# A table places the first stage's instructions, and the bias split moves from the expert stage into that stage

## The chip, the cores and the metric

The kernel runs on one core of a Trainium2 chip. The metric is the device time of one execution in microseconds; three timed runs are shown, and one more execution was profiled.

## What is computed

One layer of a diffusion trunk over 256 latent tokens and 256 context tokens of width 1024: a bidirectional chunked gated DeltaNet (8 heads of 128, chunks of 64) as the token mixer, then a mixture of 32 experts, of which each token takes 4, then a final normalisation. Everything is float32. The reference, cut to what matters here:

```python
hx = modulate(rmsnorm(x, norm1_g[i]), mx[0], mx[1])
hc = modulate(rmsnorm(ctx, norm1_g[i]), mc[0], mc[1])
o_c, s_f, s_b = bidir_gated_delta(qc, kc, vc, gc, bc, zero_state, zero_state)
o_x, _, _ = bidir_gated_delta(qx, kx, vx, gx, bx, s_f, s_b)
x = x + mx[2] * gdn_output(o_x, zx, gdn_norm_g[j], gdn_w_out[j])
hx2 = modulate(rmsnorm(x, norm2_g[i]), mx[3], mx[4]).reshape(-1, d)

def moe(h, w_r, b_r, w_gu, b_gu, w_dn, b_dn):
    ...
    for e in range(N_EXPERTS):
        y = y + comb[:, e:e + 1] * clamped_swiglu_expert(h, w_gu[e], b_gu[e], w_dn[e], b_dn[e])
```

An expert is `h @ w_gu + b_gu` (1024 to 2048), a clamped SwiGLU, and `@ w_dn + b_dn` (1024 to 1024), so its weights are 12 MiB, and all 32 experts are 384 MiB. They are read once.

## The kernel before

**First stage (the mixer).** The work is cut into operations on a head or a group of four heads, and the list `ORDER` names the order in which they are written out: `k`, `v`, `q`, `z` project the tokens for one head (matmuls L264, L265, L426 on weights that were split into a rounded part and a rest, lines 78 and 83), `um`, `ia`, `ib`, `ic` build and invert the chunks' triangular matrices, `st` is one step of the scan over chunks for four heads, `norm` and `op` make the output and add it to the tokens `x1`, `ada` computes the gates from the conditioning vector (L693). The scheduler of the language places instructions by their position in the program; an engine runs what it is given in order. `inv_c(4)` is the last part of the inverse for the second four heads: 16 small matmuls (L599), copies of their result into `y1c`, 16 more matmuls on that (L608), and copies into `U`. In a step of the scan (`step`), PE multiplies the state `St` (L624), DVE forms `R` (L634), PE forms the new values (L642) and the update (L660), DVE adds it to `St` (L666), PE multiplies within the chunk (L672), and DVE adds this to `vs` (L676, L678). The output matmuls are L756; the last row transposes of the gates, L700, end the stage. `rowG`, the gain of the second normalisation, is loaded early into memory of the pool `ep` and transposed there (L386).

**Second stage (experts).** Tokens are routed (L892 to L957), and the experts follow one after another. Each has six weight tiles of 2 MiB, four for gate and up and two for down; all 192 are loaded by `issue` on SP's queue (L780) into a ring of nine slots, seven of which reuse memory of the first stage: a load waits until the last use of what lay there. Expert 0's gate and up matmuls are L995, the down matmuls L1030. An expert with more than 64 tokens takes an additional pass. Around it, and once for each quarter of expert 0, all engines pass a block boundary (L1181, L1221), so none gets ahead of the others there.

**The bias.** The matmuls that add a bias need it as three bfloat16 parts (`bgu`, `bdn`, 96 rows). `bias(i)`, written out after the routing, loads it three times into 32 rows each (L930, on ACT's queue), and splits it with casts on ACT (L931, L934, L936) and subtractions on DVE (L932, L935).

## Time and profile before

| | us |
|---|---|
| timed runs, median (lowest to highest of 3) | 1426.8 (1426.25 to 1428.42) |
| profiled execution | 1418.68 |
| its span | 1416.9 |
| PE busy in the span | 1269.2 (90%) |
| DVE busy | 497.9 (35%) |
| ACT busy | 363.7 (26%) |
| POOL busy | 214.5 (15%) |
| HBM read | 454.05 MB, 321 GB/s over the span |

Times within the kernel are those of the profiled execution, from the span's start. A busy share is an average over two stages with different limits, so the rows below are read by stretches.

### The profile page before, as it was taken

What the parts mean: (1) busy time and instruction counts of PE and PEld (TensorE: products, weight loads), DVE (VectorE), ACT (ScalarE), POOL (GpSimd) and SP (SyncE); (2) the same over time, 40 slices, a digit from 0 to 9 for tenths busy, and PEclk for the clock granted to TensorE, in tenths of its full rate; (3) what the DMA queues carried; (4) which work ended last, traced back from release to release, by engine and by line L of the source; (5) the groups of instructions that cost most, each with busy time, mean ns of one, the idle gap of its engine ahead of it and who ended that gap; (6) DMA issues with size and microseconds to landing.
All of it is one profiled execution on the core that took longest, in us unless ns stands there. A gap on an engine that the chain in (4) does not pass through costs nothing. (4 is left out here: it accounts for less than half of the span.)

```text
span 1416.9 us, 18778 instructions
## 1 busy us (share of the span) xinstructions
PE 1269.2 (90%) x6815; PEld 629.3 (44%) x6815; DVE 497.9 (35%) x1076; ACT 363.7 (26%) x811; POOL 214.5 (15%) x204
## 2 busy tenths in 40 slices
PE   4997899889996899999899999999999899987995
PEld 2565667678753333333343334333333333332331
DVE  4569989856553121120112221121211102111123
ACT  3375453435435311111120211211111111111112
POOL 3043334315310000100000001000100001000011
PEclk9999899979998899999999999999999999999998
DMA  9633334323667699999996999999999999999992
GB/s 257 211 90 89 105 108 117 123 86 105 242 287 268 272 428 426 426 426 425 427 424 250 399 427 426 426 426 426 426 426 427 427 426 427 426 427 422 425 426 98
DMA packets 88582, 457.11 MB, mean 323 GB/s; under 512 B 7940, under 2 KB 57289, under 8 KB 63857
## 3 DMA queue, kind: packets, MB, share of 16 engines
q1 hardware_dynamic: 85392, 453.68, 79.8%
q8 instruction: 94, 1.54, 0.4%
q10 hardware_dynamic: 3041, 1.44, 0.4%
q14 instruction: 55, 0.45, 0.1%
HBM read 454.05 MB, written 1.05 MB: 321 GB/s over the span
## 5 line engine op out<-in xcount | busy, mean ns | idle before, releaser
L995 PE MATMUL psG<-w,hTe 128*64 128x512 f32 x1024 | 283.7, 620 | 42.3 <-DMA w<-in_moe_w_gu_dram 25.0
L995 PE MATMUL psU<-w,hTe 128*64 128x512 f32 x1024 | 277.9, 607 | 0.0
L1030 PE MATMUL psY<-w,aT 128*64 128x512 f32 x1024 | 225.2, 592 | 0.1
L1216 POOL TENSOR_TENSOR YAB<-y,YAB 64x512 fp32r<-64x512 f32 x62 | 78.4, 1264 | 887.5 <-ACT YAB L1215 885.2
L1211 DVE SCALAR_TENSOR_TENSOR y<-psY,cw,gate 128x512 f32<-128x512 f32 x32 | 24.0, 751 | 354.1 <-PE psY L1030 354.1
L995 PEld LDWEIGHTS psU<-w,hTe 128*64 128x64 f32 x1024 | 85.4, 141 | 134.6 <-issue 131.6
L1030 PEld LDWEIGHTS psY<-w,aT 128*64 128x64 f32 x1024 | 73.5, 137 | 140.4 <-issue 137.7
L995 PEld LDWEIGHTS psG<-w,hTe 128*64 128x64 f32 x1024 | 66.7, 137 | 147.6 <-issue 109.9
L1005 DVE TENSOR_SCALAR g<-psG 128x512 f32<-128x512 f32 x33 | 34.3, 1041 | 237.4 <-PE psG L995 232.8
L1215 ACT CAST YAB<-y 64x512 fp32r<-64x512 f32 x64 | 39.4, 616 | 291.9 <-DVE y L1211 152.9
L264 PE MATMUL pp<-hh,w 128*128 128x256 f32 (+1 forms) x240 | 86.6, 376 | 13.1 <-DVE w L78 5.1
L265 PE MATMUL pp<-hl,w 128*128 128x256 f32 (+1 forms) x240 | 84.7, 368 | 0.0
L1034 DVE TENSOR_TENSOR x<-x,psX 128x512 f32<-128x512 f32 x68 | 43.7, 683 | 108.7 <-PE psX L1089 106.8
L979 ACT ACTIVATE hTe<-psX,adac,A 128x128 f32<-128x128 f32 x128 | 48.1, 456 | 127.4 <-PE psX L977 127.4
L83 POOL TENSOR_TENSOR w<-w 128x1024 fp32r<-128x1024 f32 x24 | 57.6, 2399 | 109.0 <-ACT w L78 29.3
L977 PEld LDWEIGHTS psX<-oh,xn 128*128 128x128 f32 x512 | 59.5, 192 | 25.0 <-issue 12.2
L445 DVE SCALAR_TENSOR_TENSOR acc<-pp,colB,acc 128x508 f32<-128x508 f32 (+3 forms) x96 | 62.5, 653 | 19.7 <-ACT acc L433 18.9
L977 PE MATMUL psX<-oh,xn 128*128 128x128 f32 x512 | 65.4, 281 | 0.6 <-DVE oh L968 0.6
L264 PEld LDWEIGHTS pp<-hh,w 128*128 128x128 f32 x240 | 49.6, 207 | 24.4 <-DVE w L78 5.8
L426 PE MATMUL pp<-hh,w 128*128 128x256 f32 (+1 forms) x240 | 53.7, 352 | 0.6 <-POOL w L83 0.6
L265 PEld LDWEIGHTS pp<-hl,w 128*128 128x128 f32 x240 | 49.6, 207 | 6.1 <-issue 0.5
L1077 ACT CAST ST<-psX 128x256 fp32r<-128x256 f32 x16 | 5.9, 371 | 170.0 <-PE psX L1075 170.0
(400 smaller groups left out, 1449.7 us busy)
## 6 DMA issues: line engine op xcount, KB each, us to landing
w<-in_moe_w_gu_dram SPq DMA_DIRECT2D x128, 2048.0 KB, 19.7
w<-in_moe_w_dn_dram SPq DMA_DIRECT2D x64, 2048.0 KB, 21.1
w<-in_gdn_w_in_dram SPq DMA_DIRECT2D x32, 512.0 KB, 4.2
w<-in_ada_w_dram SPq DMA_DIRECT2D x32, 512.0 KB, 4.0
sl<-in_ada_w_dram SPq DMA_DIRECT2D x16, 512.0 KB, 5.3
w<-in_gdn_w_out_dram SPq DMA_DIRECT2D x8, 512.0 KB
xt<-in_ctx_dram SPq DMA_DIRECT2D x2, 512.0 KB
xt<-in_x_dram SPq DMA_DIRECT2D x2, 512.0 KB
```

The costliest lines, as they stand in the source:

```text
L83: eng[e2].tensor_tensor(lo, x, hi.bitcast(F32), op=ALU.subtract)
L264: T.matmul(ps, wh, xh, start=first, stop=False)
L265: T.matmul(ps, wh, xl, start=False, stop=last and not low)
L426: T.matmul(p[:, t0:512], w[1][:, k], hh[:, k, t0:512], start=False, stop=(k == 7))
L445: V.scalar_tensor_tensor(o, i, tap(j), o, op0=ALU.mult, op1=ALU.add)
L977: T.matmul(pt[:, d % 4 * n:d % 4 * n + n], xn[:, t, d * P:(d + 1) * P], oh[:, t, 0:n], start=(t == 0), stop=(t == 1))
L979: S.activation(dst[:, d, 0:n], pt[:, d % 4 * n:d % 4 * n + n], AF.Identity, scale=A2[:, d:d + 1], bias=B2[:, d:d + 1])
L995: T.matmul(ps[64 * c:64 * c + 64], hc, w[:, q * D + c * 512:q * D + (c + 1) * 512], start=(k == 0 and late), stop=(k == 7 and not late))
L1030: T.matmul(py[o:o + 64], aT[:, b, c * 64:(c + 1) * 64], w[:, n * 512:(n + 1) * 512], start=False, stop=(r == 7))
L1034: V.tensor_tensor(xs, xs, ps, op=ALU.add)
L1215: S.copy(YAB[0][r, n], y[r])
L1216: (G if e + 1 < E else V).tensor_tensor(YAB[1][r, n], y[r], YAB[0][r, n].bitcast(F32), op=ALU.subtract)
```

## The change

- **The table.** `V`, `S`, `G`, `T` and a new `SY` (SP's queue) become `Ranked` objects. Each takes a list of numbers from `RANK` (1774 for PE, 745 for DVE, 368 for ACT, 146 for POOL, 108 for SP), and each instruction of the first stage gets the next number as its place in the scheduler's list. After the stage the place is set behind all of these.
- **The bias** goes into the first stage: six operations `bias(i)` stand in `ORDER` between the last scan steps. The load is one 64 KB transfer for each (SP's queue), the casts are on DVE (30 of 32x512), the subtractions on POOL (12 of 32x512). Its buffers are the two `bx` tiles that the expert stage uses later under other names. Expert 0 no longer has its bias matmuls behind its weight matmuls.
- **rowG** is loaded with the other rows at the start, lies in the pool `gp` in place of `ep`, and is transposed in `moer`, at the end of the stage.

```diff
+class Ranked:
+    def __init__(self, tc, engine, text):
+        z = zlib.decompress(base64.b85decode(text))
+        self.tc, self.engine, self.base = tc, engine, tc.cur_priority
+        self.ranks = iter([z[i] + 256 * z[i + 1] for i in range(0, len(z), 2)])
+    def __getattr__(self, name):
+        f = getattr(self.engine, name)
+        def call(*args, **kw):
+            r = next(self.ranks, None)
+            if r is not None:
+                self.tc.cur_priority = self.base + r
+            return f(*args, **kw)
+        return call
...
-    V, S, G, T = nc.vector, nc.scalar, nc.gpsimd, nc.tensor
+    V, S, G, T, SY = (Ranked(tc, x, RANK[n]) for n, x in (("V", nc.vector), ("S", nc.scalar), ("G", nc.gpsimd),
+                                                          ("T", nc.tensor), ("SP", nc.sync)))
+    last = tc.cur_priority + 3153
...
-    rowG = ep.tile([4, 256], F32, name="rowG")
+    rowG = gp.tile([4, 256], F32, name="rowG")
...
     def moer():
         next(ag, None)
+        pt = pT()
+        for a in range(2):
+            nc.tensor.transpose(pt[:, 4 * a:4 * a + 4], rowG.rearrange("q (p a) -> q a p", a=2)[:, a], ident[0:4, 0:4])
...
+    def bias(i):
+        g, n = divmod(i, 2)
+        if not n:
+            for n_ in range(2):
+                b = A["moe_b_dn"][0] if g == 2 else A["moe_b_gu"][0][:, g * D:(g + 1) * D]
+                SY.dma_start(bx[n_][32 * g:32 * g + 32], b[:, n_ * 512:(n_ + 1) * 512])
+        x = bx[n][32 * g:32 * g + 32]
+        hi = (mk["bdn"] if g == 2 else mk["bgu"][:, g * D:(g + 1) * D])[:, n * 512:(n + 1) * 512]
+        sb = wka.tile([P, 512], BF, tag="vT", name="sb", bufs=1)[32 * g:32 * g + 32]
+        for u in range(3):
+            V.tensor_copy(hi[32 * u:32 * u + 32], x)
+            if u < 2:
+                V.tensor_copy(sb, x)
+                G.tensor_tensor(x, x, sb, op=ALU.subtract)
...
     for o_ in ORDER:
         ops[o_[0]](*o_[1:])
+    tc.cur_priority = last
...
-    for i in range(3):
-        bias(i)
...
-            gemm1(e, k, ws[k], hT[:, k, e % 2 * 64:e % 2 * 64 + 64], pg, pu, e == 0)
+            gemm1(e, k, ws[k], hT[:, k, e % 2 * 64:e % 2 * 64 + 64], pg, pu, False)
```

SP's queue at the end of the first stage. `w<-in_moe_w_gu_dram` and `w<-in_moe_w_dn_dram` are the ring's tiles, `bx` the biases, `x_...<-in_x_dram` the tokens. Before:

```order
L740 DMA w<-in_gdn_w_out_dram 128x1024 x4
L800 DMA x_3377<-in_x_dram 64x1024 x4
L809 DMA wr<-in_router_w_dram 128x4x64
L810 DMA br<-in_router_b_dram 128x32
L780 DMA w<-in_moe_w_gu_dram 128x4096
L740 DMA w<-in_gdn_w_out_dram 128x1024
L780 DMA w<-in_moe_w_gu_dram 128x4096
L740 DMA w<-in_gdn_w_out_dram 128x1024
L780 DMA w<-in_moe_w_gu_dram 128x4096 x2
L780 DMA w<-in_moe_w_dn_dram 128x4096 x2
L780 DMA w<-in_moe_w_gu_dram 128x4096 x3
```

And of the change, in the same place (L127 is the line of `Ranked` that passes a call on):

```order
L127 DMA w<-in_gdn_w_out_dram 128x1024 x5
L127 DMA w<-in_moe_w_gu_dram 128x4096 x2
L127 DMA x_3373<-in_x_dram 64x1024 x4
L127 DMA wr<-in_router_w_dram 128x4x64
L127 DMA br<-in_router_b_dram 128x32
L127 DMA bx<-in_moe_b_dn_dram 32x512 x2
L127 DMA bx<-in_moe_b_gu_dram 32x512 x2
L127 DMA w<-in_gdn_w_out_dram 128x1024
L127 DMA bx<-in_moe_b_gu_dram 32x512 x2
L127 DMA w<-in_moe_w_gu_dram 128x4096 x2
L127 DMA w<-in_moe_w_dn_dram 128x4096 x2
L127 DMA w<-in_moe_w_gu_dram 128x4096 x3
```

The ring's first two tiles moved ahead of the tokens, and six bias loads now stand ahead of the third tile. By its semaphores this third tile waits for PE's second `rowG` transpose (L922). On PE that stands here, at the very end of the first stage (`row` are the gates' row transposes, `pp<-w` the output matmuls, of which each counts as two in the trace):

```order
L127 MATMUL pp<-w,kT_642 128x512
L127 MATMUL pt<-ident,o_3717 128x128
L127 MATMUL pp<-w,kT_642 128x512 x9
L127 MATMUL pt<-ident,row_86 128x128
L922 MATMUL pt<-ident,rowG 128x4
L127 MATMUL pt<-ident,row_86 128x128
L922 MATMUL pt<-ident,rowG 128x4
L127 MATMUL pt<-ident,row_86 128x128 x2
```

Before, 12 output matmuls stood between the last transpose of `o` and the row transposes; now there are 9, and both `rowG` transposes lie among the row transposes.

DVE in the last scan steps, before (`vt`, `St`, `vs` and `R` belong to `step`):

```order
L646 TENSOR_TENSOR vt<-pm,ct 128x512
L666 TENSOR_TENSOR St_640<-St_640,pm 128x4x128 x2
L676 TENSOR_TENSOR vs_644<-vs_644,pm 128x4x128
L678 SCALAR_TENSOR_TENSOR vs_644<-pm,eg,vs_644 128x128 x4
L634 SCALAR_TENSOR_TENSOR R<-pm,neg_eg,vs_644 128x128 x4
```

And of the change, from the same instruction on:

```order
L127 TENSOR_TENSOR vt<-pm,ct 128x512
L127 CAST bdn<-bx 32x512
L127 CAST sb<-bx 32x512
L127 CAST bdn<-bx 32x512 x2
L127 CAST sb<-bx 32x512
L127 CAST bgu<-bx 32x512
L127 TENSOR_TENSOR St_636<-St_636,pm 128x4x128
L127 CAST bdn<-bx 32x512
L127 CAST sb<-bx 32x512
L127 CAST bgu<-bx 32x512
L127 TENSOR_TENSOR St_636<-St_636,pm 128x4x128
```

Six casts now stand between `vt` and the first addition to `St`, and three between the two additions; twelve more follow before the `vs` update of the next step.

PE around `inv_c(4)`, before (`W`, `U` and `y1c` belong to the inverse, `w,sc` to the gates, `hh` and `hl` to the projections):

```order
L426 MATMUL pp<-hh,w 128x256 x2
L693 MATMUL pm<-w,sc 32x512 x12
L599 MATMUL pm<-W_2623,U_645 128x32 x16
L264 MATMUL pp<-hh,w 128x256
L265 MATMUL pp<-hl,w 128x256
...
L608 MATMUL pm<-W_2623,y1c 128x32 x16
```

And of the change (a part of the projections between is left out):

```order
L127 MATMUL pm<-W_2619,U_641 128x32 x16
L127 MATMUL pm<-w,sc 32x512 x3
L127 MATMUL pp<-hh,w 128x256
L127 MATMUL pp<-hl,w 128x256
...
L127 MATMUL pp<-hh,w 128x256 x9
L127 MATMUL pp<-hl,w 128x256
L127 MATMUL pt<-ident,qb 128x128
...
L127 MATMUL pm<-W_2619,y1c 128x32 x16
```

Nine of the gate matmuls moved ahead of the scan step before it, and the projections between the two groups of 16 grew from 5 to more than 30.

## Rows read from the trace of the kernel before

**Rows 1.** The page: its head, and what DMA moved in 40 slices

```profile
span 1416.9 us, 18778 instructions
...
GB/s 257 211 90 89 105 108 117 123 86 105 242 287 268 272 428 426 426 426 425 427 424 250 399 427 426 426 426 426 426 426 427 427 426 427 426 427 422 425 426 98
```

**Rows 2.** Windows: busy time (instructions) per engine, PE clock, DMA share, GB/s

```profile
core 0: us, PE busy (x) PEld busy (x) DVE busy (x) ACT busy (x) POOL busy (x), PEclk, DMA share, GB/s
100.00:300.00 200.00, 174.77 (x1204) 132.97 (x1203) 184.69 (x374) 93.90 (x229) 67.29 (x54) 0.95 0.36 107
300.00:320.00 20.00, 16.46 (x81) 15.49 (x82) 4.20 (x7) 5.25 (x10) 3.40 (x3) 0.57 0.21 51
...
388.67:399.66 10.99, 10.98 (x84) 7.41 (x83) 5.67 (x15) 5.44 (x16) 1.26 (x1) 1.00 0.01 1
...
400.00:420.00 20.00, 19.45 (x58) 9.00 (x56) 11.08 (x26) 5.32 (x21) 2.64 (x3) 1.00 0.98 399
...
400.00:500.00 100.00, 79.56 (x380) 38.87 (x378) 34.99 (x93) 39.21 (x73) 5.16 (x5) 0.91 0.79 310
...
740.00:800.00 60.00, 54.23 (x258) 19.87 (x256) 17.10 (x30) 7.60 (x15) 5.05 (x4) 1.00 0.76 305
800.00:1380.00 580.00, 542.38 (x2542) 212.45 (x2541) 104.70 (x178) 89.51 (x189) 48.03 (x38) 0.97 1.01 426
```

**Rows 3.** Waits of PE, 430 to 800 us: total us, times, longest

```profile
PE psX L1073 <- ACTq L1181: 17.4, 1, 17.4
PE psG L995 <- DMA w<-in_moe_w_gu_dram: 6.9, 3, 3.7
```

**Rows 4.** The tile bx: its loads for `bdn`, and the wait for them

```profile
L930 ACTq DMA_DIRECT2D bx<-in_moe_b_dn_dram x3: 317/317/439, 444.9 to 448.6; - x3
...
  DMA bx<-in_moe_b_dn_dram: 9.0, 1
```

**Rows 5.** Waits of SP's queue, 355 to 490 us

```profile
SPq L780 <- DMA bx<-in_moe_b_gu_dram: 19.2, 3, 17.1
```

**Rows 6.** Timeline of SP's queue: start us, us, what

```profile
399.65 0.80 SPq L780 DMA_DIRECT2D w<-in_moe_w_gu_dram  x2
405.76 4.55 SPq L780 DMA_DIRECT2D w<-in_moe_w_dn_dram  x2
```

**Rows 7.** Timeline of PE in expert 0

```profile
434.36 1.08 PE L995 MATMUL psG<-w,hTe 128*64 128x512 f32 x4
...
442.28 1.08 PE L995 MATMUL psG<-w,hTe 128*64 128x512 f32 x4 [0.30 <-PEq L1181]
```

**Rows 8.** Timeline of PE around `inv_c(4)`; brackets: idle before, releaser

```profile
300.54 1.05 PE L693 MATMUL pm<-w,sc 128*32 128x512 f32 x4 [1.40 <-DMA w<-in_ada_w_dram]
301.52 6.00 PE L599 MATMUL pm<-W,U 128*128 128x32 f32 x32
310.52 0.58 PE L264 MATMUL pp<-hh,w 128*128 128x256 f32 x1 [3.00 <-ACT w L78]
...
311.75 6.87 PE L608 MATMUL pm<-W,y1c 128*128 128x32 f32 x32
```

**Rows 9.** Timeline of PE at the end of the first stage

```profile
408.85 10.47 PE L756 MATMUL pp<-w,kT 128*128 128x512 f32 x24
419.15 0.63 PE L700 MATMUL pt<-ident,row 128*128 128x128 f32 x4
```

**Rows 10.** Waits of PE, 20 to 419 us

```profile
PE pt L459 <- ACT kT L449: 7.1, 4, 3.8
PE pp L264 <- DVE w L78: 5.1, 3, 2.5
```

**Rows 11.** Groups by form: busy us, mean ns | idle before, releaser

```profile
L610 DVE COPY U<-W 32x512 f32<-32x512 f32 x4 | 2.5, 623 | 0.0
...
L593 DVE COPY spare<-W 32x512 f32<-32x512 f32 x4 | 1.8, 447 | 0.1
...
L653 POOL TENSOR_TENSOR St<-St,egl 128x512 f32<-128x512 f32 x24 | 24.8, 1052 | 40.0 <-PE pm L624 40.0
...
L509 ACT ACT_TABLE_LOAD x10 | 12.8, 1283 | 3.4 <-DVE kt L542 2.7 <-PE pm L506 0.6
```

More of the change, by code (lines that the diff above doesn't have):

```diff
@@ L1 @@
+import base64
+import zlib
 from contextlib import ExitStack
@@ L135, in tile_kernel @@
     rowA = ep.tile([25, P], F32, name="rowA")
-    rowG = ep.tile([4, 256], F32, name="rowG")
+    rowG = gp.tile([4, 256], F32, name="rowG")
     rowB = ep.tile([120, P], F32, name="rowB")
     rowC = ep.tile([48, P], F32, name="rowC")
-    nc.sync.dma_start(rowA[0:8], A["c"].rearrange("o (a p) -> (o a) p", p=P))
-    nc.sync.dma_start(rowA[8:16], A["c_ctx"].rearrange("(a p) -> a p", p=P))
-    nc.scalar.dma_start(rowA[16:24], A["norm1_g"].rearrange("o (a p) -> (o a) p", p=P))
-    nc.scalar.dma_start(rowA[24:25], A["gdn_norm_g"])
-    nc.scalar.dma_start(rowC, A["ada_b"].rearrange("o (a p) -> (o a) p", p=P))
+    SY.dma_start(rowA[0:8], A["c"].rearrange("o (a p) -> (o a) p", p=P))
+    SY.dma_start(rowA[8:16], A["c_ctx"].rearrange("(a p) -> a p", p=P))
+    S.dma_start(rowA[16:24], A["norm1_g"].rearrange("o (a p) -> (o a) p", p=P))
+    S.dma_start(rowG, A["norm2_g"].rearrange("o (q r) -> (o q) r", q=4))
+    S.dma_start(rowA[24:25], A["gdn_norm_g"])
+    S.dma_start(rowC, A["ada_b"].rearrange("o (a p) -> (o a) p", p=P))
     xt = ep.tile([P, 4, D], F32, name="xt")
     for i in range(2):
-        nc.sync.dma_start(xt[:, i], A["ctx"][0, i * P:(i + 1) * P, :])
-        nc.sync.dma_start(xt[:, 2 + i], A["x"][0, i * P:(i + 1) * P, :])
+        SY.dma_start(xt[:, i], A["ctx"][0, i * P:(i + 1) * P, :])
+        SY.dma_start(xt[:, 2 + i], A["x"][0, i * P:(i + 1) * P, :])
     def load_w(n):
         w = wt().rearrange("p (k n) -> p k n", k=8)
-        nc.sync.dma_start(w, A["gdn_w_in"][0, :, n * P:(n + 1) * P].rearrange("(k p) n -> p k n", p=P))
+        SY.dma_start(w, A["gdn_w_in"][0, :, n * P:(n + 1) * P].rearrange("(k p) n -> p k n", p=P))
         return w
@@ L381, in tile_kernel @@
     V.tensor_scalar(neg_eg, eg, -1.0, None, op0=ALU.mult)
-    nc.scalar.dma_start(rowG, A["norm2_g"].rearrange("o (q r) -> (o q) r", q=4))
-    pt = pT()
-    for a in range(2):
-        T.transpose(pt[:, 4 * a:4 * a + 4], rowG.rearrange("q (p a) -> q a p", a=2)[:, a], ident[0:4, 0:4])
-    S.copy(colA[:, 25:33].rearrange("p (q a) -> p a q", a=2), pt[:, 0:8].rearrange("p (a q) -> p a q", a=2))
     ectx.close()
@@ L685, in ada @@
             c0 = s * 2048 + j * 512
-            nc.scalar.dma_start(row[32 * j:32 * j + 1], A["ada_b"][:, c0:c0 + 512])
+            S.dma_start(row[32 * j:32 * j + 1], A["ada_b"][:, c0:c0 + 512])
         pa = pM()
@@ L779, in issue @@
             w = rings[i % NR].tile([P, 4096], F32, tag="w", name="w")
-            nc.sync.dma_start(w, src(i))
+            SY.dma_start(w, src(i))
             c = 2 if i % 6 < 4 else 4
@@ L799, in hclose @@
         for t, u, r in rows_of(A["x"][0]):
-            nc.sync.dma_start(x1[64 * u:64 * u + 64, t], r)
+            SY.dma_start(x1[64 * u:64 * u + 64, t], r)
     E = 32
-    mk = {}
+    mk, bx = {}, []
     def moec():
@@ L822, in moec @@
         xt("A2", [P, 8])
-        for t in "gu":
-            xp.tile([P, 512], F32, tag=t, name="bx", bufs=1)
+        bx.extend(xp.tile([P, 512], F32, tag=t, name="bx", bufs=1) for t in "gu")
     def moer():
         next(ag, None)
+        pt = pT()
+        for a in range(2):
+            nc.tensor.transpose(pt[:, 4 * a:4 * a + 4], rowG.rearrange("q (p a) -> q a p", a=2)[:, a], ident[0:4, 0:4])
+        S.copy(colA[:, 25:33].rearrange("p (q a) -> p a q", a=2), pt[:, 0:8].rearrange("p (a q) -> p a q", a=2))
         V.scalar_tensor_tensor(mk["A2"], adac[:, 4], 1.0, colA[:, 25:33], op0=ALU.add, op1=ALU.mult)
@@ L834, in moer @@
         V.tensor_tensor(mk["wr"], mk["wr"], mk["A2"].rearrange("p (k e) -> p k e", e=1).to_broadcast([P, 8, E]), op=ALU.mult)
-    ops = {"dc": decu, "moec": moec, "fin": moer, "g1": gates, "k": key, "n": knorm, "v": value, "um": umats, "ia": inv_a, "ib": inv_b, "ic": inv_c, "st": step, "q": query,
+    def bias(i):
[12 more added lines that the diff above has]
+                G.tensor_tensor(x, x, sb, op=ALU.subtract)
+    ops = {"dc": decu, "moec": moec, "fin": moer, "g1": gates, "bias": bias, "k": key, "n": knorm, "v": value, "um": umats, "ia": inv_a, "ib": inv_b, "ic": inv_c, "st": step, "q": query,
            "am": amats, "z": zgate, "ada": lambda: next(ag, None), "hclose": hclose, "norm": norm, "wo": wo, "op": oproj,
@@ L922, in tile_kernel @@
     V.scalar_tensor_tensor(posm, pp[:, 0:2 * E].rearrange("p (t e) -> p t e", e=E), 1.0, sb, op0=ALU.add, op1=ALU.mult)
-    def bias(i):
-        x = mw.tile([P, D], F32, tag=f"YAB{i % 2}", name="bx", bufs=1)[0:96]
-        hi = bdn if i == 2 else bgu[:, i * D:(i + 1) * D]
-        b = A["moe_b_dn"][0] if i == 2 else A["moe_b_gu"][0][:, i * D:(i + 1) * D]
-        for u in range(3):
-            nc.scalar.dma_start(x[32 * u:32 * u + 32], b)
-        S.copy(hi, x)
-        V.tensor_tensor(x, x, hi, op=ALU.subtract)
-        for u in (1, 2):
-            S.copy(hi[32 * u:32 * u + 32], x[32 * u:32 * u + 32])
-        V.tensor_tensor(x[64:96], x[64:96], hi[64:96], op=ALU.subtract)
-        S.copy(hi[64:96], x[64:96])
     def counts():
@@ L1185, in tile_kernel @@
                 for k in range(done, k1):
-                    gemm1(e, k, ws[k], hco[:, k], pgo, puo, e == 0)
+                    gemm1(e, k, ws[k], hco[:, k], pgo, puo, False)
                 if k1 == 8:
```

94 lines of the change are left out of this document (83 added, 11 removed).

## The prediction

> **What bounds the kernel now.** I read the page's slices first. From the middle of the span on, the DMA row stands at 426 GB/s in nearly every slice, with one dip near 740 us [rows 1]. The windows put numbers on it: 426 GB/s from 800 to 1380 us, and 305 GB/s from 740 to 800 us [rows 2]; the last slice, with 98 GB/s, is the tail. At 426.5 GB/s (the slices say 426 or 427) a 2 MiB tile (2.097 MB) takes 2.097/0.4265 = 4.92 us, and all 192 tiles go through SP's queue. So the end of the kernel is "when the weight stream gets going" plus a constant. A microsecond won before the stream saturates is kept to the end; one won on TensorE after that is not, since PE itself waits for weights by then (6.9 us on `w` between 430 and 800 us [rows 3]).
>
> The stream does not get going cleanly. From 400 to 500 us DMA moved 310 GB/s on average [rows 2]: 31.0 MB, of which the bias loads are 9 x 0.131 = 1.2 MB, so 29.8 MB or 14.2 tiles. The chain behind this is in the waits: PE waits 17.4 us, once, for ACT's sequencer at the block boundary L1181 [rows 3]; ACT spends 9.0 us of it waiting for the `bdn` bias, whose loads it issued itself between 444.9 and 448.6 us, behind 2 MiB tiles, and then it still has the casts of that bias to do [rows 4]. SP holds the next ring tile until PE has passed. There is a second hold: SP waited 17.1 us for a `bx` bias load before it could issue a further tile, because the DMA completion semaphores go round and those two tiles' turn fell on semaphores that bias loads on ACT's queue had used [rows 5].
>
> Before 419 us there is no weight stream to speak of; the mixer is bound by DVE from 100 to 300 us (185 of 200 us busy) and by PE from 360 us on, with a half-clock stretch (0.57 in the mean) between 300 and 320 us [rows 2].
>
> **The change, part by part.**
>
> *The bias leaves the expert stage.* ACT no longer has a load to wait for and PE's 17.4 us go; so does the 17.1 us hold on SP. What limits instead? `rowG` now lies in memory that the third tile of the ring reuses, and in the built program this load waits for the second `rowG` transpose, which stands among the last row transposes of the mixer. Before, this third tile was issued at 399.65 us and four tiles went out by about 410 us [rows 6]. Now tiles 3 to 9 all wait for the transposes, which before began at 419.15 us [rows 9]. Behind it on SP's queue stand the other six tiles; PE wants the third tile at 442.28 us, and it lands near 426 us, so nobody waits for this but the stream itself. I put the issue at 419.5 us and the flow at 421.2 us (the first of the four went out at 399.65 us, and 400 to 420 us then shows 399 GB/s, 20 x (1 - 399/426.5) = 1.3 us short, so about 1.6 us pass). From there nothing should stop it: expert 0 starts at 434.4 us as before, and PE takes 3.96 us a tile in its first matrices (two tiles, 32 matmuls, between 434.36 and 442.28 us [rows 7]), so slots come free faster than a tile lands. By 500 us the new stream has moved (500 - 421.2) x 0.4265 = 33.6 MB against 29.8 MB: 3.8 MB, or **-8.9 us**. I keep -7 to -10 for the latency. This holds for an unchanged mixer; each microsecond by which the mixer ends earlier or later comes on top, one for one. Without the `rowG` hold the tiles could flow from 401 us, and the gain would be some 20 us more; the change does not get that. The dip at 740 us stays: 60 x (1 - 305/426.5) = 17 us, with PE waiting for weights on both sides of it.
>
> *The table, around `inv_c(4)`.* Before, PE waits 1.40 us before the last of the gate matmuls L693, does them, then the 32 L599 matmuls in 6.00 us, then waits 3.00 us for a weight cast, and after five projection matmuls does 32 L608 matmuls in 6.87 us [rows 8]. Now L599 comes before the last gate matmuls, some 35 projection matmuls stand between L599 and L608, and the ACT cast is queued ahead of the inverse's copies. The 1.40 and 3.00 us are covered: -4.4 us. Whether the narrow matmuls then run at the higher clock is open; at twice the clock 12.87 us would be 6.4 us less. Ends: 0 and -10.8 us. I take **-4.4 us**, since these narrow matmuls themselves stand before and in the low stretch and are not removed.
>
> *The table, elsewhere.* The largest waits of PE in the mixer that aren't counted above are 7.1 us for `kT` and 5.1 us for weight casts on DVE [rows 10], 12.2 us together. The table pulls projections and casts earlier, but DVE, busy 185 of 200 us up to 300 us, has no more room than before, and what PE gains there it hands on to the same scan. I take 3 of the 12.2 us, ends 0 and -6.1 (half of it): **-3 us.** Four more activation-table loads at 1.283 us each [rows 11] lie on ACT, which is busy 94 of 200 us [rows 2]: nothing; if ACT's cover were gone, 5.1 us.
>
> *The bias goes into the mixer's tail.* The six loads of 64 KB stand on SP's queue ahead of the third tile, which waits for the end of the mixer anyway: nothing (without that cover, 6 x 0.40 us of issue, half of the 0.80 us of two tiles [rows 6], 2.4 us). The bias matmuls of expert 0 move ahead of its weights: nothing, since the biases are cast by then. But 30 DVE casts of 32x512 and 12 POOL subtractions go between the last scan steps, 21 of the casts before the `vs` update that stood at 399.66 us. No row shows this cast; DVE copies of 32x512 take 447 ns at one place and 623 ns at another [rows 11]. So 21 x 0.45 = 9.4 us to 21 x 0.62 = 13.0 us, against 10.99 - 5.67 = 5.3 us of idle DVE in 388.67 to 399.66 us [rows 2]: +4.1 to +7.7 us on that update. PE waits for it, but 3 pairs of output matmuls that ran after the last transpose (24 in 10.47 us [rows 9]) now run earlier: 6 x 0.436 = -2.6 us. Ends +1.5 and +5.1 us; **+3 us**, near the middle, as neither copy row is nearer. A rule speaks against this part: the Trainium skill, "GPSIMD Engine Reference", 1. Specifications, says that GpSimd shares its SBUF interfaces with VectorE and contends with VectorE instructions in a two-port mode or with two SBUF inputs. The two copy rows differ as it would have it, though no row names the cause. By the rule the casts cost the upper end and the sum would be 2 us worse.
>
> Sum: -8.9 - 4.4 - 3 + 3 = -13.3 us. The profiled execution took 1418.68 us (span 1416.9 us and 1.8 us around it), so it would be 1405.4 us; the timed runs have a median of 1426.8 us, 8.1 us above it, for which the profile shows no cause, and I carry that over: 1426.8 - 13.3 = **1413.5 us**.
>
> **Rivals.**
> *A, the above* (gain of 7 to 20 us): 0.60.
> *B, the clock.* Wide projections among the narrow matmuls keep the clock at 2.4 GHz from 300 to 320 us: another 6.4 us, and the scan behind starts earlier, so that half of the 12.2 us goes too: -8.9 - 10.8 - 6.1 + 3 = -22.8 us, 1404 us. For it: where projections run, from 100 to 300 us, the clock is 0.95 in the mean [rows 2]. Against: the narrow matmuls remain, and DVE is the bound before them. The Trainium skill, "TensorE: Matmul & The Clock Gate", What's actually happening, says that the low clock is the default and activity lifts it; the trace agrees in so far as the narrow stretch is the one that shows 0.57. 0.14.
> *C, the mixer gives it back.* The table wins nothing and the casts cost the upper end: -8.9 + 5.1 = -3.8 us, 1423 us. For it: DVE has no slack before 300 us. 0.11.
> *D, slower.* One mechanism: each cast-subtract-cast round is serial, DVE in order waiting for POOL, with one `sb` buffer for both halves. A round is two casts and a POOL operation (1052 ns for a 128x512 one [rows 11]), 2 x 0.62 + 1.05 = 2.3 us; eight before the `vs` update are 18.4 us, less 5.3 us idle, +13.1 us; the stream is held until the mixer ends, so it all counts, and PE has run out of output matmuls to fill the gap with: 1426.8 - 8.9 + 13.1 = 1431.0 us if the table wins nothing. It decides if the last transposes come later than 419.15 + 8.9 = 428.1 us. Before, the tiles of 400 to 420 us were a cushion that hid such a delay; the new hold takes it away. 0.10.
> *E, no change:* the stall is gone, but the stream stops elsewhere, e.g. a longer dip at 740 us gives the 9 us back, and the mixer is even. 0.05.
>
> **How the numbers follow.** 1413.5 us is A's. The range reaches from 4 us below B (1400 us) to between C and E (1425 us) and leaves out the far part of B (0.03), D and E: under 2 in 10. A difference within 0.2% (2.9 us) is about what a measurement of this kernel can't tell from no change. Faster: A, B and C, 0.85, less 0.02 for C's edge; same: E and edges, 0.06; slower: D, 0.11 with E's edge.
>
> **What would show it.** Right: no wait of PE at L1181 over 1 us; DMA at 426 GB/s without a hole from about 2 us after the `rowG` transposes; those transposes at 415 us or so; no tile between the second and that moment (a nearly empty DMA from 385 to 415 us apart from biases); PE without the 3.00 us wait near 310 us. Wrong: a hole in DMA after 425 us (then the stall has only moved), `rowG` transposes after 428 us with DVE waiting for POOL at the bias casts (D), or before 405 us at a clock near 1.0 throughout 300 to 320 us (B).

## The result

The changed kernel takes 1401.74 us (median of 4 runs, 1399.83 to 1404.81), the kernel before, run beside it, 1426.53 us (4 runs, 1424.0 to 1428.42). The ratio is 0.9829 [0.9805, 0.9854]: 24.8 us faster. The forecast was 1413.5 us, 13.3 us faster, so the direction and the range held and the size is about half of what came. From one profiled execution to the other it is 1418.68 to 1402.79 us, or -15.9 us.

**The stream.** The page of the changed kernel, the lines that answer to [rows 1]:

```profile
span 1401.0 us, 18799 instructions
...
GB/s 259 214 106 90 107 104 108 151 130 119 175 90 429 426 425 426 427 426 426 427 402 267 403 425 427 425 427 426 427 426 427 427 426 426 427 427 419 427 419 84
```

A slice is 35.0 us. The thirteenth, from 420 us on, is the first at full rate and no slice behind it has a hole, apart from the dip at 740 us. Before, the four slices from 354 to 496 us stood at 242 to 287 GB/s. The windows, with the columns of [rows 2]:

```profile
300.00:320.00 20.00, 18.14 (x148) 16.80 (x148) 8.37 (x17) 11.18 (x34) 10.06 (x7) 0.93 0.35 106
...
380.00:400.00 20.00, 15.54 (x59) 8.03 (x56) 17.75 (x43) 8.06 (x28) 12.28 (x10) 0.91 0.00 0
...
400.00:500.00 100.00, 94.72 (x469) 44.63 (x469) 28.28 (x89) 27.54 (x56) 8.14 (x8) 1.00 0.89 372
...
740.00:800.00 60.00, 56.93 (x274) 21.86 (x272) 13.36 (x25) 9.17 (x20) 5.11 (x4) 1.00 0.87 350
```

DMA moves nothing from 380 to 400 us, then 372 GB/s from 400 to 500 us (310 before). From 300 to 320 us the granted clock is 0.93 (0.57 before) and PE does 148 instructions in place of 81. The dip now lies over 700 to 800 us: 358 GB/s in its first 40 us and 350 in the last 60 lose 6.4 + 10.8 = 17.2 us, as the 17 us before.

SP's waits from 340 to 470 us, and below its timeline:

```profile
SPq L127 <- PE pt L922: 32.3, 1, 32.3
```

```profile
411.16 0.82 SPq L127 DMA_DIRECT2D w<-in_moe_w_gu_dram  x2
412.10 0.98 SPq L127 DMA_DIRECT2D w<-in_moe_w_dn_dram  x2
```

As forecast, the third tile waits for the `rowG` transposes (L922), 32.3 us long, and goes out at 411.16 us; four tiles are out by about 413 us. The 17.1 us hold of [rows 5] is gone. PE's waits from 419 to 800 us, for [rows 3]:

```profile
PE psG L127 <- DMA w<-in_moe_w_gu_dram: 12.5, 6, 2.8
...
PE psG L127 <- PEq L1277: 3.8, 20, 0.3
```

The 17.4 us at the block boundary are now 20 passes of 0.3 us at most, and PE waits longer for weights instead: the stream is the bound.

**The end of the first stage.** PE's timeline, for [rows 8] and [rows 9]:

```profile
292.88 4.08 PE L127 MATMUL pm<-W,U 128*128 128x32 f32 x32 [0.37 <-ACT W L127]
...
304.52 3.65 PE L127 MATMUL pm<-W,y1c 128*128 128x32 f32 x32
...
402.37 7.89 PE L127 MATMUL pp<-w,kT 128*128 128x512 f32 x18
410.09 0.27 PE L127 MATMUL pt<-ident,row 128*128 128x128 f32 x1
410.30 0.28 PE L922 MATMUL pt<-ident,rowG 4*128 4x4 f32 x1
```

The two groups of 32 narrow matmuls take 7.73 us, before 12.87. Both waits of [rows 8] are gone. The row transposes begin at 410.09 us, 9.06 us earlier. DVE's timeline in the last scan steps:

```profile
371.35 0.69 DVE L127 TENSOR_TENSOR vt<-pm,ct 128x512 f32<-128x512 f32 x1
372.07 0.61 DVE L127 CAST bdn<-bx 32x512 bf16<-32x512 f32 x1
...
374.63 0.42 DVE L127 CAST bdn<-bx 32x512 bf16<-32x512 f32 x1 [1.05 <-POOL bx L127]
...
390.78 1.48 DVE L127 CAST sb<-bx 32x512 bf16<-32x512 f32 x1
...
392.29 0.69 DVE L127 TENSOR_TENSOR vs<-vs,pm 128x512 f32<-128x512 f32 x1
```

The last `vt` comes at 371.35 us, 17.3 us earlier; of this the bias casts behind it give 8.2 us back. The tile `bx` shows their prices (ns: least, median, most):

```profile
L127 POOL TENSOR_TENSOR bx<-bx,sb x12: 1145/1150/1600, 373.3 to 403.8; 32x512 f32<-32x512 f32 x12
...
L127 DVE CAST sb<-bx x12: 404/416/1481, 372.7 to 403.2; 32x512 bf16<-32x512 f32 x12
```

A cast is 416 ns in the median, below both copies of [rows 11]; a subtraction is 1150 ns; and DVE waits for POOL between them, 1.05 us in the line above. DVE's waits from 365 to 410 us hold nine such, 5.2 us together:

```profile
DVE bgu L127 <- POOL bx L127: 2.6, 5, 0.8
DVE bdn L127 <- POOL bx L127: 2.6, 4, 1.1
```

### The profile page after: what moved, and what is told of

It is laid out like the page before. It is cut to its first block, busy times and chain, and to the rows that moved or that the text cites. A ratio compares the mean times of both kernels' runs of the same rounds, so it can differ in the third digit from the quotient of the medians.

```text
span 1401.0 us, 18799 instructions
## 1 busy us (share of the span) xinstructions
PE 1272.3 (91%) x6815; PEld 625.7 (45%) x6815; DVE 496.3 (35%) x1100; ACT 356.9 (25%) x803; POOL 230.3 (16%) x216
## 3 DMA queue, kind: packets, MB, share of 16 engines
HBM read 453.27 MB, written 1.05 MB: 324 GB/s over the span
## 5 line engine op out<-in xcount | busy, mean ns | idle before, releaser
L127 PE MATMUL psG<-w,hTe 128*64 128x512 f32 x1024 | 284.9, 620 | 48.8 <-DMA w<-in_moe_w_gu_dram 31.8
L127 PE MATMUL psU<-w,hTe 128*64 128x512 f32 x1024 | 278.5, 606 | 0.0
L127 PE MATMUL psY<-w,aT 128*64 128x512 f32 x1024 | 226.0, 594 | 0.0
L127 POOL TENSOR_TENSOR YAB<-y,YAB 64x512 fp32r<-64x512 f32 x62 | 79.1, 1275 | 881.7 <-ACT YAB L127 879.3
L127 DVE SCALAR_TENSOR_TENSOR y<-psY,cw,gate 128x512 f32<-128x512 f32 x32 | 24.0, 750 | 363.6 <-PE psY L127 363.6
L127 PEld LDWEIGHTS psU<-w,hTe 128*64 128x64 f32 x1024 | 86.1, 140 | 134.0 <-issue 128.9
L127 PE MATMUL pp<-hh,w 128*128 128x256 f32 (+1 forms) x480 | 136.1, 360 | 8.5 <-DVE acc L127 6.8
L127 PEld LDWEIGHTS psG<-w,hTe 128*64 128x64 f32 x1024 | 67.3, 138 | 155.6 <-issue 112.1
L127 PEld LDWEIGHTS psY<-w,aT 128*64 128x64 f32 x1024 | 73.3, 137 | 141.3 <-issue 138.5
L127 DVE TENSOR_SCALAR g<-psG 128x512 f32<-128x512 f32 x33 | 34.3, 1040 | 237.4 <-PE psG L127 232.8
L127 ACT CAST YAB<-y 64x512 fp32r<-64x512 f32 x64 | 39.4, 616 | 293.4 <-DVE y L127 153.9
L127 PEld LDWEIGHTS pp<-hh,w 128*128 128x128 f32 x480 | 88.4, 201 | 27.0 <-issue 6.2
L127 PE MATMUL pp<-hl,w 128*128 128x256 f32 (+1 forms) x240 | 84.4, 366 | 0.0
L127 DVE TENSOR_TENSOR x<-x,psX 128x512 f32<-128x512 f32 x68 | 43.8, 684 | 109.8 <-PE psX L127 109.8
L127 ACT ACTIVATE hTe<-psX,adac,A 128x128 f32<-128x128 f32 x128 | 48.2, 457 | 128.9 <-PE psX L127 128.9
L127 POOL TENSOR_TENSOR w<-w 128x1024 fp32r<-128x1024 f32 x24 | 57.7, 2402 | 104.9 <-PE pm L127 28.8
L127 PEld LDWEIGHTS psX<-oh,xn 128*128 128x128 f32 x512 | 59.5, 191 | 25.0 <-issue 12.9
L127 DVE SCALAR_TENSOR_TENSOR acc<-pp,colB,acc 128x508 f32<-128x508 f32 (+3 forms) x96 | 62.3, 652 | 11.3 <-ACT acc L127 10.7
L127 PE MATMUL psX<-oh,xn 128*128 128x128 f32 x512 | 65.4, 281 | 0.6 <-DVE oh L127 0.6
L127 ACT CAST ST<-psX 64x256 fp32r<-64x256 f32 (+1 forms) x48 | 17.7, 369 | 182.4 <-PE psX L127 182.0
L127 PEld LDWEIGHTS pp<-hl,w 128*128 128x128 f32 x240 | 49.4, 206 | 6.3 <-issue 0.9
```

Of the source, the lines that this page charges most:

```text
L127: return f(*args, **kw)
```

## The experiments

All times stand against the kernel before, timed on the same chip (its medians were 1424.2 to 1425.7 us there).

**The table alone.** The changed kernel, with the bias and `rowG` as they were before:

```diff
-    rowG = gp.tile([4, 256], F32, name="rowG")
+    rowG = ep.tile([4, 256], F32, name="rowG")
...
     def bias(i):
-        g, n = divmod(i, 2)
...
+        skip(SY, 2 if i % 2 == 0 else 0)
+        skip(V, 5)
+        skip(G, 2)
...
+    for i in range(3):
+        bias(i)
```

> The table alone: bias split, bias loads on ACT's queue and the early rowG transposes stay as before the change. Theory A (each part moves the start of the weight stream, and every microsecond of that start counts once): the vt update that stood at 388.7 us comes at 371 us as in the changed kernel, the tail is as long as before since no casts lie in it, the row transposes come at 402 us, the 17 us stall at the block boundary stays: 17 us faster than before, about 1409 us. Theory B (the bias split is the larger part, the table only brings what is seen in the end of the mixer): 7 to 9 us faster, about 1418 us.

1406.72 us, 0.9885 [0.9845, 0.9926]. The waits of PE from 400 to 800 us show the old stall:

```profile
PE psX L127 <- ACTq L1289: 18.0, 1, 18.0
```

The row transposes begin at 404.63 us, 14.5 us earlier than before, and the span is 14.0 us shorter: a microsecond of the mixer counts once here, although the stall is still there. The medians differ by 19.0 us, since the profiled execution of before was a quick one (below).

**The bias and `rowG` without the table.** `Ranked` no longer sets a place:

```diff
             r = next(self.ranks, None)
-            if r is not None:
-                self.tc.cur_priority = self.base + r
             return f(*args, **kw)
...
-    tc.cur_priority = last
```

> The bias split in the first stage and the late rowG transposes, with the order of the program in place of the table. Theory A: mixer as slow as before the change, vt at 388 us, the casts delay the row transposes to 421 to 426 us, the third tile goes out behind them, the stall is gone: by 500 us 31.2 to 33 MB have come instead of 29.8, so 3 to 7 us faster than before, about 1420 to 1423 us. Theory B: 15 to 17 us faster, about 1410 us, since PE's 17.4 us wait is what was removed.

1408.95 us, 0.9884 [0.9848, 0.9921]. No wait at the boundary is left, and the row transposes begin at 418.57 us, within 0.6 us of before: span 1407.4 us, -9.5 us. The time is near theory B's, but its reason, 15 to 17 us from the stall alone, is not what the trace shows: PE's timeline has what the table was credited with:

```profile
297.06 4.96 PE L125 MATMUL pm<-W,U 128*128 128x32 f32 x32 [0.37 <-ACT W L125]
...
308.71 3.65 PE L125 MATMUL pm<-W,y1c 128*128 128x32 f32 x32
```

The groups of `inv_c(4)` stand here as in the changed kernel, with projections between them. In the two traces, `rowG`'s transposes left aside, the first 2323 of the stage's 2496 matmuls come in the same order, and up to 347 us the instructions of DVE, ACT and POOL and the loads of SP do too. So something other than the table reorders the stage.

**`rowG` early.** The changed kernel with `rowG` back in pool `ep`, transposed early; bias and table stay:

```diff
-    rowG = gp.tile([4, 256], F32, name="rowG")
+    rowG = ep.tile([4, 256], F32, name="rowG")
...
+    pt = pT()
+    for a in range(2):
+        nc.tensor.transpose(pt[:, 4 * a:4 * a + 4], rowG.rearrange("q (p a) -> q a p", a=2)[:, a], ident[0:4, 0:4])
...
     def moer():
...
-        pt = pT()
-        for a in range(2):
-            nc.tensor.transpose(pt[:, 4 * a:4 * a + 4], rowG.rearrange("q (p a) -> q a p", a=2)[:, a], ident[0:4, 0:4])
```

> The changed kernel with rowG transposed early as before the change, so that the third tile does not wait for the end of the mixer. Theory A (the hold costs tiles): the third tile goes out at about 380 us, the ring is full when expert 0 starts, DMA has no hole of 30 us before 411 us; until PE frees the first slot at about 431 us nine tiles can be there in place of 5.7, so 3.3 tiles or 13 to 16 us faster than the changed kernel, 1386 to 1389 us. Theory C (the other waits of these tiles, for St, o and the last output matmuls, end as late as the transposes): within 3 us of the changed kernel.

1394.23 us, 0.9791 [0.9751, 0.9831]. Its slowest run (1398.23 us) is below the changed kernel's fastest (1399.83 us); the gain over it is 7.5 us, half of what was expected. (The intervals of the two ratios overlap; the spans of the two profiles differ by 7.5 us too, 1393.5 against 1401.0 us.) SP's timeline:

```profile
393.24 0.82 SPq L127 DMA_DIRECT2D w<-in_moe_w_gu_dram  x2
399.49 7.03 SPq L127 DMA_DIRECT2D w<-in_moe_w_dn_dram  x2
412.45 1.29 SPq L127 DMA_DIRECT2D w<-in_moe_w_gu_dram  x3
```

The third tile goes out 17.9 us earlier and not at once: SP waits 12.2 us for matmuls of the scan and 11.2 us for `St` first, and 6.3 us for `kT` after it. So other memory of the mixer holds the tiles in `rowG`'s place (387 GB/s from 400 to 500 us). The prediction had put "some 20 us" on this hold.

**No subtraction.** The 12 `sb` casts and the 12 POOL subtractions are left out, so that all three parts of a bias hold its rounded value:

```diff
             V.tensor_copy(hi[32 * u:32 * u + 32], x)
             if u < 2:
-                V.tensor_copy(sb, x)
-                G.tensor_tensor(x, x, sb, op=ALU.subtract)
+                next(V.ranks, None)
+                next(G.ranks, None)
```

> The changed kernel without the casts to sb and the subtractions on POOL: 18 casts of 32x512 in place of 30, none waiting for POOL (all three parts of a bias are then its rounded value). Theory A (the rounds through POOL stretch the tail of the scan by 10 us between vt and the vs update, and the row transposes follow): vs update 5 to 7 us earlier, row transposes at 403 to 405 us, 5 to 7 us faster than the changed kernel, about 1395 us. Theory D (PE is full there with output matmuls anyway, so the casts are hidden): row transposes within 2 us of 410 us, no difference in time.

1391.90 us, 0.9775 [0.9732, 0.9817], some 10 us below the changed kernel where 5 to 7 were expected. PE's timeline and, below it, the tile `bx`:

```profile
402.89 0.27 PE L127 MATMUL pt<-ident,row 128*128 128x128 f32 x1
```

```profile
L127 DVE CAST bgu<-bx x12: 407/416/1515, 374.5 to 385.9; 32x512 bf16<-32x512 f32 x12
```

The row transposes come 7.2 us earlier. From the last `vt` to them it is 31.9 us, and 31.3 us in the kernel without any casts there (the table alone), so 18 casts cost 0.6 us. It is the rounds of cast, subtraction and cast that cost. One cast of 1515 ns remains although nothing is subtracted; POOL is at another operation then. POOL's timeline and DVE's, and below them POOL's in the changed kernel, around its cast of 1.48 us:

```profile
383.52 1.27 POOL L127 TENSOR_TENSOR x<-x,xg 128x512 f32<-128x512 f32 x1 [4.01 <-DVE f L127]
383.56 2.81 DVE L127 CAST bgu<-bx 32x512 bf16<-32x512 f32 x4
```

```profile
390.48 1.50 POOL L127 TENSOR_TENSOR x<-x,xg 128x512 f32<-128x512 f32 x1
```

This is the rule of all long casts. Over all profiled executions, 48 of the 240 casts on DVE took 560 to 1515 ns; each of them began while POOL was in a `TENSOR_TENSOR`, an operation on two tiles (here `x`, `St`, `bx` or `dec`), and ended 0.28 us after it. None of the other 192, 395 to 420 ns each, began with more than 0.1 us of such an operation to go.

**Early loads, late split**, with the table and, in a second kernel, without it. `rowG` is early; the biases are loaded where the change loads them and split behind the routing, and expert 0 has its bias matmuls behind its weights again:

```diff
     def bias(i):
...
-        for u in range(3):
-            V.tensor_copy(hi[32 * u:32 * u + 32], x)
-            if u < 2:
-                V.tensor_copy(sb, x)
-                G.tensor_tensor(x, x, sb, op=ALU.subtract)
+        skip(V, 5)
+        skip(G, 2)
...
     softmax()
+    for i in range(3):
+        bsplit(i)
```

> The changed kernel with the table, with rowG transposed early, the 64 KB bias loads where the change puts them, and most of the split (casts on DVE, subtractions on POOL) behind the routing, beside expert 0, whose bias matmuls come after its weights as before the change. Theory A (three separate things move the start of the weight stream: the table, the casts in the tail, the hold by rowG; the stall hangs on the loads and not on the place of the split): row transposes at 403 to 406 us as with the table alone, third tile at 385 us, no wait of PE over 3 us at the block boundary, 6 to 9 us faster than the kernel with early rowG, 1385 to 1388 us. Theory F (the split itself stalls expert 0 wherever it stands behind the routing): PE waits 10 us or more for bgu or bdn in expert 0, the stream is held again, not faster than 1394 us.

> The same without the table: order of the program. Theory A: the mixer ends as in the bias-only kernel less its casts, row transposes at 410 to 413 us, 6 to 9 us slower than with the table, 1392 to 1396 us; so the table is worth that much here. Theory G (the scheduler's own order loses nothing once the program has changed): within 3 us of the kernel with the table.

With the table 1404.48 us, 0.9854 [0.9833, 0.9875]; without it 1420.17 us, 0.9982 [0.9966, 0.9999]. The first misses its expectation: the split is off the mixer, but PE's waits show a new one,

```profile
PE psG L127 <- DVE sm L127: 9.4, 1, 9.4
```

since most casts stand ahead of the routing's last steps `sm` on DVE. That is theory F's time with a wait for another tile. The second misses both its theories (it has the same wait, 9.5 us) and shows PE's timeline as before:

```profile
304.18 7.04 PE L125 MATMUL pm<-W,U 128*128 128x32 f32 x32
315.44 6.87 PE L125 MATMUL pm<-W,y1c 128*128 128x32 f32 x32
```

Here, with `rowG` early and no table, the order of `inv_c(4)` is the old one: the first 2420 of the stage's 2496 matmuls come as in the kernel before. With `rowG` early the table is worth 15.7 us.

**The kernel before, profiled again, twice.**

> The kernel before, profiled once more, since its timed runs lie between 1419 and 1428 us and its profiled execution at the lower end of that. Theory H (the half-clock stretch of PE in the mixer has a different length in each execution): the row transposes come later than 419 us by as much as this execution is longer than 1418.7 us, the stall at the block boundary stays 17 us. Theory I (the bias loads behind the 2 MiB tiles land at different times): the row transposes at 419 us, the stall longer by the difference.

> The same once more, with the same two theories: H, the difference lies in the mixer, ahead of the row transposes; I, it lies in the stall behind them.

1423.52 and 1428.34 us; the row transposes begin at 421.09 and 425.87 us. Windows of the first execution and of the second:

```profile
0.00:100.00 100.00, 77.11 (x478) 49.66 (x478) 54.53 (x184) 42.04 (x96) 27.37 (x29) 0.95 0.70 196
```

```profile
0.00:100.00 100.00, 77.36 (x439) 50.18 (x440) 51.87 (x181) 38.62 (x88) 27.35 (x29) 0.88 0.68 192
```

The same program does 478 PE instructions in its first 100 us at a clock of 0.95, and 439 at 0.88. In both executions L608 takes 6.87 us. Neither theory holds whole: of the 4.8 and 9.7 us by which their spans exceed the first one's, 1.9 and 6.7 us lie ahead of the row transposes (H) and 2.8 and 2.9 us behind them (I; the stall is 19.3 and 18.2 us), and H's half-clock stretch is not where the second one loses most, but the first 100 us: its first `y1c` matmul comes 4.7 us later.

**Only `rowG` late.** The kernel before, with nothing changed but `rowG`, which is loaded at the start, lies in `gp` and is transposed at the end:

```diff
-    rowG = ep.tile([4, 256], F32, name="rowG")
+    rowG = gp.tile([4, 256], F32, name="rowG")
...
+    nc.scalar.dma_start(rowG, A["norm2_g"].rearrange("o (q r) -> (o q) r", q=4))
...
-    nc.scalar.dma_start(rowG, A["norm2_g"].rearrange("o (q r) -> (o q) r", q=4))
-    pt = pT()
-    for a in range(2):
...
     def moer():
...
+        pt = pT()
+        for a in range(2):
...
```

> The kernel before with rowG alone moved as in the change (loaded at the start, held in the other pool, transposed at the end of the mixer); no table, bias as before. Theory J (without the two early transposes the scheduler itself finds the order that the table writes down, so this move carries the mixer's gain): PE's order is that of the changed kernel up to the last scan steps, vt at 371 to 381 us, row transposes at 404 to 411 us, the third tile right behind them, the 17 us stall stays: 5 to 15 us faster than before, 1410 to 1420 us. Theory K (the table carries the gain): vt at 388 us or later, row transposes at 419 us or later, the third tile 20 us later than before: not faster than before.

1413.10 us, 0.9921 [0.9895, 0.9946]. The row transposes begin at 401.51 us, 17.6 us earlier than before, with no table and no bias moved: theory J, and 2.5 us earlier than J had it. But behind them it loses 8.7 to 11.6 us against the three executions of before; PE's waits from 400 to 800 us and ACT's from 375 to 480 us:

```profile
PE psX L1072 <- ACTq L1180: 27.3, 1, 27.3
```

```profile
ACT bgu L930 <- DMA bx<-in_moe_b_gu_dram: 11.7, 2, 8.7
ACT bdn L930 <- DMA bx<-in_moe_b_dn_dram: 9.4, 1, 9.4
```

The tiles now go out together at the end of the mixer, and ACT's bias loads queue behind them: the stall, which J had at 17 us, grows from 17.4 to 27.3 us. That the loads wait behind the tiles is read off the order of the issues; no run separates it.

**Casts on ACT.** The kernel with `rowG` early, 18 of the 30 casts on ACT:

```diff
         for u in range(3):
-            V.tensor_copy(hi[32 * u:32 * u + 32], x)
+            next(V.ranks, None)
+            nc.scalar.copy(hi[32 * u:32 * u + 32], x)
```

> The changed kernel with early rowG transposes and with the 18 casts into bgu and bdn on ACT in place of DVE; the 12 casts to sb stay on DVE, the 12 subtractions on POOL. Theory A (casts on DVE stretch the tail by some 7 us): row transposes at 404 to 408 us in place of 412 us, 5 to 8 us faster than with all casts on DVE, 1387 to 1390 us. Theory L (ACT waits for POOL in its order, ahead of its copies for the scan, and stretches the tail as much): row transposes at 410 us or later, 1393 us or more.

1395.92 us, 0.9790 [0.9763, 0.9816], the same as with the casts on DVE. ACT now waits for POOL; its waits from 360 to 430 us:

```profile
ACT bgu L944 <- POOL bx L127: 5.2, 6, 1.3
```

The number of DVE casts isn't the price; the serial rounds are.

**The bias in the tail, no table, `rowG` early.** The edit of the run without the table and that of `rowG` early together:

```diff
-            if r is not None:
-                self.tc.cur_priority = self.base + r
...
-    rowG = gp.tile([4, 256], F32, name="rowG")
+    rowG = ep.tile([4, 256], F32, name="rowG")
```

> The bias split in the first stage without the table and with the early rowG transposes as before the change, so that neither of the two can change the mixer's order. Theory J: PE's order is that of the kernel before, vt at 388 us or later, row transposes at 421 to 428 us, the stall gone and the third tile at 400 to 408 us: 12 to 18 us slower than the same with the table, 1406 to 1412 us. Theory K (the bias-only kernel had its 8 us at vt by the luck of the clock): vt at 381 us again.

1413.17 us, 0.9910 [0.9878, 0.9943]. The first 2338 of the stage's 2496 matmuls come as in the kernel before, and the timeline around the inverse is the old one:

```profile
318.49 6.87 PE L125 MATMUL pm<-W,y1c 128*128 128x32 f32 x32
```

The last `vt` comes at 401.77 us, so theory K is out. The row transposes, at 437.5 us, come later than J had them (421 to 428 us); the profiled execution is the slowest of the four (1419.47 us).

**All loads and casts one scan step earlier**, with the table and `rowG` early:

```diff
+        tc.cur_priority = SY.base + 2740
+        for g in range(3):
+            for n in range(2):
...
+        tc.cur_priority = SY.base + 2800
+        for g in range(3):
+            for u in range(3):
+                for n in range(2):
...
+                    nc.vector.tensor_copy(hi[32 * u:32 * u + 32], x)
```

> The kernel with the table and the early rowG transposes, with the six bias loads ahead of the ring's first tiles and the split (30 casts on DVE, 12 subtractions on POOL) one scan step earlier, so that all casts stand between the R of that step and the last vt, and none between vt and the vs updates. Theory A (what costs is casts between vt and the vs updates, where PE has no other work than output matmuls): row transposes at 404 to 408 us instead of 412.6 us, 4 to 8 us faster than with the casts in the tail, 1386 to 1390 us. Theory M (the scan is one chain, so casts stretch it by the same amount in any of its last steps): vt later by 7 to 10 us, row transposes within 2 us of 412 us, 1392 to 1397 us.

1402.31 us, 0.9851 [0.9816, 0.9886], 8 us slower than with the casts in the tail. The last `vt` comes 19.3 us later (392.80 against 373.51 us), of which the mixer's start explains 4.1, and only 10.1 us come back behind it. Theory A is out, and it is worse than theory M's 1392 to 1397 us: there was no slack one step earlier, the scan is one chain.

## Why the prediction was half right

The mixer can be cut at three points that every profile has: the first `y1c` matmul (`inv_c(0)`), the last one (`inv_c(4)`), and the last `vt`. The times below are differences of starts, in us, one execution each; the last column is the span behind the start of the row transposes.

| kernel | table, `rowG`, casts in tail | first `y1c` | to last `y1c` | to last `vt` | to row transposes | behind |
|---|---|---|---|---|---|---|
| before | no, early, no | 195.0 | 123.2 | 70.5 | 30.5 | 997.8 |
| before again 1 | no, early, no | 195.1 | 125.7 | 69.8 | 30.5 | 1000.6 |
| before again 2 | no, early, no | 199.7 | 125.5 | 70.2 | 30.5 | 1000.7 |
| late split, no table | no, early, no | 195.2 | 126.7 | 70.8 | 30.5 | 998.0 |
| bias in tail, no table | no, early, yes | 200.3 | 124.7 | 76.8 | 35.8 | 979.1 |
| only `rowG` late | no, late, no | 192.1 | 114.5 | 64.4 | 30.6 | 1009.4 |
| bias and `rowG` | no, late, yes | 195.3 | 116.8 | 68.6 | 37.9 | 988.8 |
| changed kernel | yes, late, yes | 191.8 | 116.1 | 63.5 | 38.7 | 990.9 |
| table alone | yes, early, no | 195.4 | 113.7 | 64.3 | 31.3 | 998.3 |
| `rowG` early | yes, early, yes | 192.3 | 116.8 | 64.4 | 38.7 | 981.3 |

**Right: the stall and the stream's new start.** The forecast was -8.9 us with the mixer unchanged. The run of bias and `rowG` without the table had that case by the sum alone (the last `vt` 8.0 us earlier, the way from it to the row transposes 7.4 us longer): the row transposes 0.6 us earlier, and its span was 9.5 us shorter. In the last column the kernels without the stall and with `rowG` late have 988.8 and 990.9 us, the kernel before 997.8 to 1000.7: 7 to 12 us. The hold by `rowG`, the dip of 17 us and the rule that a microsecond of the mixer counts once were also right; with only `rowG` late that rule failed, since the stall grew. What was not right is the price of the hold, some 20 us: without it the last column falls to 979.1 to 981.7 us in the kernels without the stall (`rowG` early, casts on ACT, all loads one step earlier, bias in tail without table), 7 to 12 us less.

**Failed: who reorders the mixer.** "The table, around `inv_c(4)`" and "The table, elsewhere" gave the reorder to the table. The column to the last `y1c` falls into two groups, 113.7 to 117.3 us (the three table runs that are not listed gave 117.3 us, the one without subtraction 114.6) and 123.2 to 126.7 us, and they don't part by the table. Without it, a late `rowG` gives the first and an early one the second: take `rowG`'s two small transposes out of the program's beginning, and the scheduler finds the other order itself. In the traces the two orders part ten matmuls behind the place of these transposes. I had compared only before with after, where both edits are made, and the order shows what moved but not which edit moved it. The table keeps the good order when `rowG` is early (15.7 us there; with the casts in the tail 17 by the ratios, 18.9 by the medians). In the change as it was made, all that it is seen to do is to place the casts better: from the last `y1c` to the row transposes the casts cost 11.5 us without it (68.6 + 37.9 against 64.4 + 30.6) and 7.2 us with it (63.5 + 38.7), so some 4 us. Of the other 4.2 us up to the row transposes, 0.7 lie between the two `y1c` points and 3.5 before the first, where both run the same order. These 3.5 us arise from 27 to 42 us and go with a lower clock: windows of the run without the table and of the changed kernel,

```profile
20.00:40.00 20.00, 16.76 (x111) 9.54 (x110) 9.80 (x31) 5.71 (x11) 4.71 (x2) 0.74 1.02 259
...
20.00:40.00 20.00, 17.38 (x137) 10.59 (x137) 11.17 (x33) 6.30 (x12) 4.73 (x2) 0.91 1.12 286
```

In the kernel before it is 0.91, 0.91 and 0.72, with the first `y1c` at 195.0, 195.1 and 199.7 us. The medians with and without the table still differ by 7.2 us (1401.74 and 1408.95 us); what makes up the rest of that is not shown.

**Mis-sized: the mixer's gain, -7.4 us.** It was -17.3 us at the last `vt`: 3.2 before the first `y1c`, 7.1 to the last one, 7.0 behind it. The 3.2 us belong to the new order as well: among executions with a clock of 0.91 from 20 to 40 us, the first `y1c` comes at 195.0 to 195.2 us in the old order (three) and at 191.8 to 192.3 us in the new (four). Windows of the kernel before, cut at the first `y1c`, at L599, at the end of L608 and at the last `vt`:

```profile
195.00:301.50 106.50, 94.40 (x789) 72.57 (x788) 95.06 (x195) 46.38 (x111) 34.14 (x34) 0.98 0.39 120
301.50:318.60 17.10, 14.10 (x73) 13.94 (x71) 4.20 (x7) 3.94 (x7) 3.40 (x3) 0.54 0.11 30
318.60:388.67 70.07, 66.65 (x609) 54.94 (x608) 40.49 (x106) 34.28 (x86) 29.93 (x49) 0.97 0.54 176
```

And of the changed kernel, at the same points:

```profile
191.80:292.90 101.10, 94.49 (x784) 71.71 (x782) 90.23 (x189) 45.63 (x111) 34.32 (x34) 0.98 0.41 126
292.90:308.20 15.30, 15.30 (x104) 13.57 (x105) 8.59 (x19) 6.19 (x12) 9.35 (x7) 0.78 0.24 65
308.20:371.35 63.15, 61.04 (x579) 49.40 (x579) 37.52 (x103) 32.77 (x82) 22.40 (x45) 1.00 0.61 193
```

Ahead of `inv_c(4)` PE is as busy as before but idle 6.6 us in place of 12.1. Within it 31 more matmuls (104 against 73) fit into 1.8 us less, without an idle moment and at a clock of 0.78 for 0.54. Behind it 30 fewer are left (579 against 609), where PE is the bound: PE's time there is 5.6 us less. Some 4 us of this are the moved matmuls (with only `rowG` late, 580 matmuls took 62.56 us at 0.97, the clock of before), the rest goes with the clock, 1.00 for 0.97. The forecast counted the waits that were covered (4.4 us) and missed the other half: what fills a wait is gone from where it stood. It also took "-4.4 us" against the clock, "since these narrow matmuls themselves stand before and in the low stretch". This was rival B's step: of its 6.4 us, 5.1 came (12.87 to 7.73 us). L608 took 3.65 to 3.70 us in every run of the new order and 6.87 us in every run of the old one. That agrees with the Trainium skill, "TensorE: Matmul & The Clock Gate", What's actually happening, by which activity lifts the clock from its low default; here wide projections run right ahead of L608.

**Mis-sized: the casts, +3 us (ends 1.5 and 5.1).** They cost 8.2 us from `vt` to the row transposes (38.7 against 30.5). The term counted DVE's time for 21 casts, 447 to 623 ns each. They take 416 ns, so this part was too dear, and the run without subtractions shows that 18 of the casts cost 0.6 us. What costs is rival D's mechanism, cast, subtraction and cast in series with DVE waiting (5.2 us of waits for POOL), at half of D's 13.1 us: 38.7 - 31.9 = 6.8 us. The term had left POOL out. The rule drawn from the Trainium skill, "GPSIMD Engine Reference", 1. Specifications (GpSimd and VectorE contend for SBUF), is borne out by the 48 long casts, each of which began under a POOL operation. Its price is the smaller part: in the changed kernel four casts are long, by 3.2 us together, and without subtractions two, by 1.3 us.

**Failed: the offset.** "For which the profile shows no cause, and I carry that over" added 8.1 us to the profiled time. The changed kernel has no such offset: 1402.79 us profiled and 1401.74 us in the median. The offset was the profiled execution of before itself, the quickest of three: 1418.68, 1423.52 and 1428.34 us, in the table 195.0 to 199.7 us to the first `y1c` and 123.2 to 125.7 us to the last. This is most of the 8.9 us by which the medians differ more than the two profiles (24.8 against 15.9). Seven timed runs of before on one chip spread from 1419.01 to 1428.38 us.

The errors partly cancelled in the pair of profiles (-15.9 us against -13.3): the mixer's -17.3 for -7.4, the casts' +8.2 for +3, and behind the row transposes -6.9 for -8.9, since before's first profile was short there too (997.8 us).

**A better kernel than both** is the changed one with `rowG` early: 1394.23 us (1395.92 us with casts on ACT). It keeps the table's order and frees the third tile's memory.

**Open.** What decides the clock from 20 to 40 us, 0.72 to 0.91 in one program. Which part of the `rowG` edit tips the scheduler over: the two transposes, the copy behind them on ACT and the memory pool always moved together.
